# A two-layer trunk on one core: layer 0 gets four seven-product pairs and modulation vectors 2 to 5 as VectorE dot products

## The chip, the cores and the metric

The kernel runs on one core of one Trainium2 chip. The time is device microseconds of one execution. TensorE (PE) multiplies; VectorE (DVE) and ScalarE (ACT) work on the results, GpSimd (POOL) and SyncE (SP) mostly issue transfers.

## What is computed

Two layers over T = 640 tokens, 128 of context and 512 of latent, D = 1024, feed-forward width 4096. Each layer takes six modulation vectors from two conditioning vectors, `c` for latent tokens and `c_ctx` for context tokens:

```python
mod = silu(c)[None] @ w_mod[l] + b_mod[l]           # the same with c_ctx
sh1, sc1, g1, sh2, sc2, g2 = split(mod, 6)          # vectors 0 to 5
h = rmsnorm(x, norm1_g) * (1 + sc1) + sh1
branches = attention, convolution, pooling, gated unit   # all from h @ w_in
merged = sum(sigmoid(h @ w_gate[i] + b_gate[i]) * (branches[i] @ w_branch[i]))
x = x + g1 * (merged @ w_out)
h = rmsnorm(x, norm2_g) * (1 + sc2) + sh2
x = x + g2 * (square(relu(h @ w_mlp_in)) @ w_mlp_out)
```

So vector 2 is first needed at the end of the mixers, vectors 4 and 3 at the second norm, vector 5 by the MLP's output.

## The kernel before

Activations lie with channels on the partitions and tokens along the columns, in tiles of 128 x 640; TensorE takes them in two halves of 320 columns (`HALVES`). Every operand is split into a high and a low part: ScalarE copies to the high part (L240), VectorE subtracts (L241). One k-step of a product is three matmuls per half: high by high, high by low, low by high (`step`, L362). An output tile (`mtile`) is eight k-steps, 48 matmuls, or four, 24, for a half slab.

Weights come in slabs of 128 x 1024 in the order of `ORDER`, by SyncE's queue into a ring of four `raw` tiles; `use` takes the next slab, and keeps the splits of three ahead. TensorE and SyncE run in the order in which the code is written (`manual_schedule`). VectorE does too from the convolution's taps to the second gate tile of gate(1) (`byhand`); elsewhere a scheduler orders VectorE and ScalarE by priorities, which `later` shifts.

A layer runs: input projections; attention, woven on TensorE with two convolution inputs and gate(0) as filling (`fill`, `_weave`); the gated unit's projection `sgu_v` and branch(0); gate(3), branch(3), gate(2), branch(2), gate(1), branch(1); the output projection; the MLP. The convolution's 31 taps (L973) are spread over the gates as VectorE work, and its norm (`conv_out`, with sums over channels on TensorE, L414) falls into gate(1). The gate activation is line 1132 (ScalarE), the gate product line 1144 (VectorE). In attention the score maximum is line 848, the exponent 849, the normalising 850 and 851; the transposed probabilities arrive in `pt` (L857), which in attention is one bank, and are split by L240 and L241.

Modulation vectors 0 and 1 of layer 0 are made at the start. Its vectors 2 to 5 are made by `mod_steps`, on TensorE: 128 matmuls (L447) and 16 transposes (L454), handed out by `tick` in the gates and branches between gate(3) and branch(1). The vectors of layer 1 are made by `mod_dots` on VectorE during layer 0's MLP: 48 blocks, each with two dots of 1024 elements (L490) against a transposed slab of `w_mod`; `side` holds such a generator, `tick` moves it one block and `flush` runs it out.

The MLP of layer 1 (`fast_mlp`) computes 13 pairs of input tiles by a seven-product scheme (L653): eight block products become seven, at the price of sums and differences. The weights' sums are made by `Feed`, the activations' differences of quarters `ta` and `tb` by VectorE at L627 to L638, early, while TensorE has plain tiles. The MLP of layer 0 is plain, in four blocks of eight input tiles.

## Time and profile before

| | us |
|---|---|
| median of three runs | 2318.97 (2317.82 to 2321.76) |
| the profiled execution | 2326.15 |
| its span | 2324.4 |
| TensorE busy | 2254.2 (97%) |
| VectorE busy | 1655.0 (71%) |
| ScalarE busy | 856.4 (37%) |

Every stretch and duration below is of the profiled execution, which took 7.2 us more than the median. A row that is busy for 50 of 50 us shows an engine without a gap; since matmuls overlap, the distance from start to start tells what one costs. The same holds for VectorE, whose rows without dependence overlap somewhat. In a row's end, "[0.82 <-ACT h L240]" is the idle time before it and what ended it.

### The profile page before, as it was taken

To read this page: it belongs to the slowest core of one execution; us is meant where nothing else is said; L and a number is where in the kernel's file an instruction comes from. 1 tells how busy PE (TensorE), PEld (TensorE's weight loads), DVE (VectorE), ACT (ScalarE), POOL (GpSimd) and SP (SyncE) were. 2 spreads that over 40 slices of the span, in tenths; PEclk is the share of its full clock that TensorE was granted. 3 is DMA by queue.
4 is the path that set the end of the run, shared out by engine and by line. 5 is a ranking of instruction groups with operands and counts; after the bars stand their busy time and mean duration, and the time that the engine had idled before them with its cause. 6 is when DMAs were issued, how large, how long until landed. Compare 5 with 4: busy or idle time off the path is not lost.

```text
span 2324.4 us, 36290 instructions
## 1 busy us (share of the span) xinstructions
PE 2254.2 (97%) x15050; PEld 2182.7 (94%) x15050; DVE 1655.0 (71%) x2557; ACT 856.4 (37%) x1296; POOL 70.4 (3%) x188
## 2 busy tenths in 40 slices
PE   6999999999999999999999999999999999999997
PEld 5989899989999999999998898999999999999987
DVE  6676457678777776766477773687897788777776
ACT  5455342222335332222254553422224453232233
POOL 1100000000000000000011000000000000000001
PEclk9999999999999999999999999999999999999999
DMA  7421122333343444444354212222222432222223
GB/s 285 113 84 60 63 70 99 133 136 136 126 138 127 154 154 146 151 148 146 108 175 107 78 46 69 73 78 64 65 76 92 150 109 65 73 85 89 73 91 110
DMA packets 77253, 252.43 MB, mean 109 GB/s; under 512 B 11808, under 2 KB 12832, under 8 KB 76960
## 3 DMA queue, kind: packets, MB, share of 16 engines
q1 hardware_dynamic: 66592, 224.56, 29.9%
q0 software_dynamic: 9920, 24.89, 3.8%
q8 instruction: 118, 1.93, 0.3%
q10 hardware_dynamic: 576, 0.66, 0.1%
q14 instruction: 47, 0.39, 0.1%
HBM read 238.65 MB, written 10.75 MB: 107 GB/s over the span
## 4 chain that ended last, share of the span: by engine, by line
PE 66%; issue 24%; DVE 6%; ACT 2%; DMA 1%; POOL 0%; SPq 0%; DVEq 0%; ACTq 0%; POOLq 0%
PE ps L362 44%; PE ph L362 5%; PE pt L653 4%; DVE l L241 2%; PE sc L653 2%; PE pt L857 1%; PE sc L846 1%; PE po L865 1%; PE sc L362 1%; ACT h L240 1%; PE po L653 1%; PE sc L1031 1%; DMA st<-in_w_mod 1%; PE pt L447 1%; PE sc L414 1%
## 5 line engine op out<-in xcount | busy, mean ns | idle before, releaser
L362 PE MATMUL ps<-h,h 128*128 128x320 f32 x5296 | 1119.3, 310 | 12.8 <-ACT gx L1132 4.7
L362 PEld LDWEIGHTS ps<-h,h 128*128 128x128 f32 x5296 | 862.7, 188 | 31.9 <-ACT h L240 12.5
L362 PE MATMUL ps<-h,l 128*128 128x320 f32 x3408 | 835.7, 309 | 0.0
L240 ACT ACTIVATE h<-raw 128x1024 fp32r<-128x1024 f32 x337 | 357.2, 1060 | 976.7 <-PE ps L362 658.8
L362 PEld LDWEIGHTS ps<-h,l 128*128 128x128 f32 x3408 | 585.6, 188 | 0.0
L241 DVE TENSOR_TENSOR l<-raw,h 128x1024 fp32r<-128x1024 f32 x337 | 411.6, 1222 | 217.5 <-ACT h L240 217.1
L362 PE MATMUL ps<-l,h 128*128 128x320 f32 x1520 | 384.6, 308 | 0.0
L362 PEld LDWEIGHTS ps<-l,h 128*128 128x128 f32 x1520 | 263.9, 188 | 0.3
L973 DVE SCALAR_TENSOR_TENSOR cv<-cv,cw,cv 128x655 f32<-128x655 f32 x240 | 215.9, 899 | 6.1
L554 DVE SCALAR_TENSOR_TENSOR x<-ps,mod,x 128x128 f32<-128x128 f32 (+2 forms) x260 | 99.8, 434 | 117.9 <-PE ps L362 117.8
L362 PE MATMUL ph<-h,h 128*128 128x320 f32 x768 | 179.6, 318 | 0.0
L362 PEld LDWEIGHTS ph<-h,h 128*128 128x128 f32 x768 | 129.1, 188 | 7.2
L240 ACT ACTIVATE h<-tmp 128x640 fp32r<-128x640 f32 (+1 forms) x92 | 67.5, 737 | 138.7 <-DVE tmp L1311 79.9
L362 PE MATMUL ph<-h,l 128*128 128x320 f32 x384 | 118.5, 309 | 0.0
L362 PE MATMUL ps<-bo,h 128*128 128x320 f32 x512 | 96.5, 309 | 1.8 <-DVE mg L1144 1.8
L241 DVE TENSOR_TENSOR l<-pt,h 128x512 fp32r<-128x512 f32 x84 | 57.9, 689 | 41.5 <-ACT h L240 41.3
L362 PEld LDWEIGHTS ps<-bo,h 128*128 128x128 f32 x512 | 80.2, 188 | 5.1 <-DVE mg L1144 2.4
L241 DVE TENSOR_TENSOR l<-tmp,h 128x640 fp32r<-128x640 f32 x92 | 74.9, 816 | 8.3 <-ACT h L240 8.3
L240 ACT ACTIVATE h<-pt 128x512 fp32r<-128x512 f32 x84 | 50.3, 599 | 77.1 <-PE pt L857 70.8
L490 DVE SCALAR_TENSOR_TENSOR junk<-raw,sw 128x1024 f32<-128x1024 f32 x48 | 58.8, 1224 | 25.4 <-DMA raw<-in_w_modt 25.2
L653 PE MATMUL pt<-h,h 128*128 128x320 f32 x260 | 71.4, 309 | 2.6 <-DVE tmp L659 2.6
L362 PEld LDWEIGHTS ph<-h,l 128*128 128x128 f32 x384 | 72.1, 188 | 0.0
(300 smaller groups left out, 2573.9 us busy)
## 6 DMA issues: line engine op xcount, KB each, us to landing
raw<-in_slabs SPq DMA_DIRECT2D x324, 512.0 KB, 3.6
raw<-in_w_modt SPq DMA_DIRECT2D x48, 512.0 KB, 3.7
md<-in_w_mod SPq DMA_DIRECT2D x32, 512.0 KB, 4.4
q<-qd POOLq DMA_DIRECT2D x18, 256.0 KB, 3.1
st<-in_w_mod SPq DMA_DIRECT2D x8, 512.0 KB, 9.7
raw<-in_w_mod SPq DMA_DIRECT2D x8, 512.0 KB, 7.1
x<-in_x SPq DMA_DIRECT2D x8, 320.0 KB, 6.0
qd<-h POOLq DMA_DIRECT2D x8, 320.0 KB, 9.1
```

The source lines that it names most:

```text
L240: act.activation(h, src, AF.Copy)
L241: (eng or vec).tensor_tensor(lo, src, _f(h), ALU.subtract)
L362: pe.matmul(v[:, c0:c1] if half is None else v, w_[:, kk, :], x_[:, c0:c1], start=first and pi == 0, stop=last and pi == 2)
L414: pe.matmul(v[:, c0:c1], ones, src[:, c0:c1], start=True, stop=True)
L447: pe.matmul(t[32 * q:32 * q + 32], sv3[:, 2 * kp + i, :], rr[i][j], start=kp == 0, stop=kp == 3)
L490: vec.scalar_tensor_tensor(out, w, 0.5, s3[s], ALU.mult, ALU.mult, accum_out=dst[:, c, s:s + 1])
L554: vec.scalar_tensor_tensor(xc[:, c0:c1], v[:, c0 - b0:c1 - b0], gv[:, c, s:s + 1], xc[:, c0:c1], ALU.mult, ALU.add)
L653: pe.matmul(v, w_[:, k0 + k, :], x_, start=k == 0 and pi == 0, stop=k == 3 and pi == 2)
L846: pe.matmul(v[:, c0:c1], lq, kk[:, SEQ + c0:SEQ + c1], start=pi == 0, stop=pi == 1)
L857: pe.transpose(pt[:, qt * P:(qt + 1) * P], parts[hd, qt][:, j * P:(j + 1) * P], ident)
L865: pe.matmul(po, vt[:, 1 + j, hd // 4, :], halves[hd, j][pi], start=j == 0 and pi == 0, stop=j == 4 and pi == 1)
L973: vec.scalar_tensor_tensor(y, b[:, j:j + CO], cw[:, c * CONV_K + j:c * CONV_K + j + 1], y, ALU.mult, ALU.add)
```

## The change

Four things are changed.

1. `mod_steps` is removed. Layer 0's vectors 2, 4, 3, 5 are made by `mod_dots`, in 32 blocks. For layer 0 a block is two dots of 512 into a small pair, an addition of the pair, and one dot of 1024 (there is no `junk` tile for a second one). Two ticks stand behind each of two convolution inputs and eight gate tiles in `fill`, so in attention; one in each product of branch(0) and, as before, in the later gates. While VectorE is ordered by hand (`hold`), ticks do nothing; the rest follows in gate(1).
2. Layer 0's MLP is `paired_mlp`: 24 input tiles plain, each with half a slab of output products behind it, then four seven-product pairs (`PLAIN = (24, 6)`). Layer 1 keeps its 13 pairs and its early differences; layer 0 makes them (`sums`) behind the plain part, after the dots of layer 1 are flushed and their room is closed.
3. In layer 0 the square of the relu moves from VectorE to ScalarE, and the residual of the MLP's output is added in two pieces (128 and 512 columns) instead of three.
4. The scratch for dynamic transfers is halved.

```diff
-FAST = (1,)
+PLAIN = (24, 6)
...
+    for j in range(4, PLAIN[l]):
+        r += [("i", j), ("h", j // 4 - 1, j % 4)]
+    for b, p, fs in PAIRS[l]:
+        r += [("i", 4 * b + 2 * p + i) for i in range(2)] + [("h", *f) for f in fs]
+    return r + 2 * [("f", 3, m) for m in range(8)]
...
-    def mod_steps(l, g, mk):
...
+    def mod_dots(l, mp, vs, src, junk=None):
...
         for i, (n, c) in enumerate(blocks):
             wn = fetch(*blocks[i + 1]) if i + 1 < len(blocks) else None
+            dst = mod3(l, vs[n])
+            if junk:
+                dot(junk(), w, s3[0], dst[:, c, 0:1])
+            else:
+                acc = small(2)
+                for hf in range(2):
+                    cs = slice(512 * hf, 512 * hf + 512)
+                    dot(tmp(512), w[:, cs], s3[0][:, cs], acc[:, hf:hf + 1])
+                vec.tensor_tensor(dst[:, c, 0:1], acc[:, 0:1], acc[:, 1:2], ALU.add)
+            dot(w, w, s3[1], dst[:, c, 1:2])
...
-        while side:
+        while side and not hold[0]:
...
+    def paired_mlp(l, h, ss1, ab, fslot, relu2, es):
...
+        for j in range(4, PLAIN[l]):
+            b, i = divmod(j, 4)
+            v = relu2(_run(mtile(use("i", j), h)))
+            fs_.setdefault(b, []).append(v)
+            tick()
+            if keep and j == 4:
+                quarters = sums()
+            w = use("h", b - 1, i)
+            for m in (2 * i, 2 * i + 1):
+                out_plain(w, m, fs_[b - 1])
+                if m % 2 or j % 2:
+                    tick()
+        if not keep:
+            flush()
+            dots.close()
+            open_room()
...
+        ta, tb = quarters or sums()
...
+                if l == 0:
+                    side.append(mod_dots(0, mx, (2, 4, 3, 5), "w_modt0"))
                 def fill():
                     for c in range(2, 4):
                         ys.append((yield from conv_in(l, c, h, cv)))
+                        for _ in range(2):
+                            tick()
                     for m in range(KC):
                         yield from gate(0, m, h, gs, True)
+                        for _ in range(2):
+                            tick()
...
+                hold[0] = True
...
                         _run(gate(1, m, h, gs))
+                        hold[0] = m < 2
...
+                if l + 1 < DEPTH:
+                    act.activation(r, r, AF.Square)
+                else:
+                    vec.tensor_tensor(r, r, r, ALU.mult)
...
-    nc = _bacc.Bacc("TRN2", target_bir_lowering=False, num_devices=1, dynamic_dma_scratch_size=4096)
+    nc = _bacc.Bacc("TRN2", target_bir_lowering=False, num_devices=1, dynamic_dma_scratch_size=2048)
```

Three places show how the order of the instructions moves. A row is the line, the operation, what it writes and reads, and its shape; numbers behind names tell tiles apart. The lines of the changed file differ from those of before: L238 is the split, L446 a dot, L460 the addition of a pair, L861 the score maximum, L863 and L864 the normalising.

VectorE in attention of layer 0, from the 21st score maximum (`sm` from `sc`) to the next, before:

```order
L848 TENSOR_REDUCE sm427_2123<-sc426_2118 128x1
L881 TENSOR_TENSOR bo217_1218<-tmp383_1924,bo216_1217 128x512
L241 TENSOR_TENSOR l432_2139<-pt430_2133,h431_2138 128x512
L848 TENSOR_REDUCE sm439_2162<-sc438_2157 128x1
L241 TENSOR_TENSOR l435_2149<-raw401_2000,h434_2148 128x1024
L850 RECIPROCAL sm428_2124<-sm428_2124 128x1
L241 TENSOR_TENSOR l444_2178<-pt442_2172,h443_2177 128x512
```

Nothing but attention's own steps and one weight split stands between the maxima.

The same place after the change:

```order
L861 TENSOR_REDUCE sm449_2175<-sc448_2170 128x1
L460 TENSOR_TENSOR mod0_78<-sm456_2200 128x1
L446 SCALAR_TENSOR_TENSOR raw419_2043,mod0_78<-raw419_2043,sw298_1551 128x1024
L446 SCALAR_TENSOR_TENSOR tmp497_2361,sm495_2358<-raw459_2207,sw298_1551 128x512
L238 TENSOR_TENSOR l454_2191<-pt452_2185,h453_2190 128x512
L460 TENSOR_TENSOR mod0_78<-sm460_2209 128x1
L446 SCALAR_TENSOR_TENSOR raw455_2198,mod0_78<-raw455_2198,sw298_1551 128x1024
L238 TENSOR_TENSOR l465_2219<-raw423_2052,h464_2218 128x1024
L894 TENSOR_TENSOR bo217_1218<-tmp397_1958,bo216_1217 128x512
L861 TENSOR_REDUCE sm469_2232<-sc468_2227 128x1
```

Two dots of 1024, one of 512 and two additions of pairs have moved between the maxima; the split of `pt` (`l454`) comes behind the first two dots.

VectorE at the end of the convolution in layer 0, from the last sum of the taps (`c`, needed by TensorE's sum over channels) to the squares, before:

```order
L983 TENSOR_TENSOR c944_5898<-c944_5898,cv900_5459 128x655
L1212 TENSOR_SCALAR cw_83<-cols1_81 128x124
L241 TENSOR_TENSOR l965_6054<-raw952_5966,h964_6053 128x1024
L988 TENSOR_TENSOR cv716_3795<-cv716_3795,sc958_6033 128x655
L988 TENSOR_TENSOR cv754_4190<-cv754_4190,sc958_6033 128x655
L988 TENSOR_TENSOR cv856_5038<-cv856_5038,sc958_6033 128x655
L988 TENSOR_TENSOR cv900_5459<-cv900_5459,sc958_6033 128x655
L460 TENSOR_TENSOR mod0_78<-tmp951_5964 128x8 x2
L422 TENSOR_TENSOR sq959_6037<-sq959_6037,sq960_6040 128x655
```

Here the only foreign rows are the two small additions (L460) of `mod_steps`.

The same place after the change:

```order
L996 TENSOR_TENSOR c993_5944<-c993_5944,cv962_5553 128x655
L1226 TENSOR_SCALAR cw_83<-cols1_81 128x124
L460 TENSOR_TENSOR mod0_78<-sm1061_6345 128x1
L446 SCALAR_TENSOR_TENSOR raw1051_6277,mod0_78<-raw1051_6277,sw298_1551 128x1024
L1001 TENSOR_TENSOR cv810_4008<-cv810_4008,sc1012_6081 128x655
L1001 TENSOR_TENSOR cv841_4382<-cv841_4382,sc1012_6081 128x655
L1001 TENSOR_TENSOR cv925_5157<-cv925_5157,sc1012_6081 128x655
L1001 TENSOR_TENSOR cv962_5553<-cv962_5553,sc1012_6081 128x655
L446 SCALAR_TENSOR_TENSOR tmp1071_6412,sm1070_6411<-raw1060_6343,sw298_1551 128x512
L446 SCALAR_TENSOR_TENSOR tmp1072_6414,sm1070_6411<-raw1060_6343,sw298_1551 128x512
L419 TENSOR_TENSOR sq1013_6085<-sq1013_6085,sq1014_6088 128x655
```

Those additions have gone; a dot of 1024 has moved ahead of the subtraction of the mean (L1001) and two of 512 ahead of the squares (L419).

VectorE in layer 0's MLP at the evictions of two output tiles of a block (`x` from `ps`), before:

```order
L554 SCALAR_TENSOR_TENSOR x1024_6581<-ps1427_9428,mod0_78,x1024_6581 128x128
L554 SCALAR_TENSOR_TENSOR x1024_6581<-ps1427_9428,mod0_78,x1024_6581 128x192
L554 SCALAR_TENSOR_TENSOR x1024_6581<-ps1427_9428,mod0_78,x1024_6581 128x320
L241 TENSOR_TENSOR l1432_9488<-raw1424_9422,h1431_9487 128x1024
L490 SCALAR_TENSOR_TENSOR junk1447_9671,mod1_79<-raw1440_9606,sw1195_7571 128x1024
L490 SCALAR_TENSOR_TENSOR raw1440_9606,mod1_79<-raw1440_9606,sw1195_7571 128x1024
L554 SCALAR_TENSOR_TENSOR x1025_6582<-ps1433_9491,mod0_78,x1025_6582 128x128
L554 SCALAR_TENSOR_TENSOR x1025_6582<-ps1433_9491,mod0_78,x1025_6582 128x192
L554 SCALAR_TENSOR_TENSOR x1025_6582<-ps1433_9491,mod0_78,x1025_6582 128x320
```

The evictions have splits and dots between them, and no other work.

After the change, VectorE at the end of the plain part, up to the last split of `ta`:

```order
L630 TENSOR_TENSOR tmp1658_10491<-h1147_6761,h1148_6762 128x320
L607 TENSOR_TENSOR tmp1655_10482<-tmp1655_10482,h1140_6754 128x320
L238 TENSOR_TENSOR l1652_10475<-tmp1650_10470,h1651_10474 128x640
L608 TENSOR_TENSOR tmp1655_10482<-tmp1657_10484,tmp1655_10482 128x320
L238 TENSOR_TENSOR l1654_10479<-tmp1647_10461,h1653_10478 128x640
L610 TENSOR_TENSOR tmp1657_10484<-tmp1657_10484,tmp1656_10483 128x320
L631 TENSOR_TENSOR tmp1658_10491<-tmp1658_10491,tmp1655_10482 128x320
L632 COPY tmp1658_10491<-tmp1657_10484 128x320
L238 TENSOR_TENSOR l1660_10496<-tmp1658_10491,h1659_10495 128x640
L238 TENSOR_TENSOR l1662_10500<-tmp1655_10482,h1661_10499 128x640
```

The differences (L605 to L632) and their splits now run up to `l1662`.

TensorE there after the change: the end of the first product of the first pair (`pt`), and the start of the second (`po`), which reads the splits `h1637` to `l1662`.

```order
L677 MATMUL pt1663_10503<-h1139_6753,h1620_10394 128x320
L677 MATMUL pt1663_10503<-h1140_6754,h1620_10394 128x320
L677 MATMUL pt1663_10503<-h1139_6753,l1621_10395 128x320
L677 MATMUL po1665_10518<-h1637_10436,h1622_10398 128x320
L677 MATMUL po1665_10518<-l1638_10437,h1622_10398 128x320
L677 MATMUL po1665_10518<-h1637_10436,l1623_10399 128x320
L677 MATMUL po1665_10518<-h1645_10457,h1622_10398 128x320
```

Between the end of `pt` and the rows of `po` no other product stands in TensorE's order.

## Rows read from the trace of the kernel before

**Rows 1.** The page, part 1: busy time, share of the span, and instructions of each engine.

```profile
PE 2254.2 (97%) x15050; PEld 2182.7 (94%) x15050; DVE 1655.0 (71%) x2557; ACT 856.4 (37%) x1296; POOL 70.4 (3%) x188
```

**Rows 2.** Busy by stretch: both layers' MLP; PE, PEld, DVE, ACT, POOL, clock, DMA, GB/s.

```profile
800.00:850.00 50.00, 50.00 (x343) 50.00 (x342) 35.50 (x53) 17.47 (x22) 0.00 (x0) 1.00 0.49 151
1900.00:1950.00 50.00, 50.00 (x343) 50.00 (x343) 46.67 (x86) 20.18 (x26) 0.00 (x0) 1.00 0.25 78
```

**Rows 3.** Line 447, the modulation matmuls: nanoseconds (least, median, most), first and last start.

```profile
L447 PE MATMUL pt<-md,silu x128: 592/605/617, 385.5 to 608.7; 128*32 128x512 f32 x128
```

**Rows 4.** Lines 1132 and 1144 in layer 0 and layer 1: first and last start.

```profile
L1132 ACT ACTIVATE gx<-ps,bgh x24: 774/778/782, 372.2 to 648.1; 128x640 f32<-128x640 f32 x24
L1144 DVE SCALAR_TENSOR_TENSOR gx<-gx,ps x24: 812/816/822, 459.4 to 675.9; 128x640 f32<-128x640 f32 x24
...
L1132 ACT ACTIVATE gx<-ps,bgh x24: 774/777/782, 1528.9 to 1787.2; 128x640 f32<-128x640 f32 x24
L1144 DVE SCALAR_TENSOR_TENSOR gx<-gx,ps x24: 814/817/822, 1610.9 to 1815.0; 128x640 f32<-128x640 f32 x24
```

**Rows 5.** Timeline of VectorE (start, length): dot of 1024, split of 640, next dot.

```profile
823.91 1.22 DVE L490 SCALAR_TENSOR_TENSOR junk<-raw,sw 128x1024 f32<-128x1024 f32 x1
...
825.05 0.82 DVE L241 TENSOR_TENSOR l<-tmp,h 128x640 fp32r<-128x640 f32 x1
825.79 1.22 DVE L490 SCALAR_TENSOR_TENSOR raw<-raw,sw 128x1024 f32<-128x1024 f32 x1
```

**Rows 6.** Timeline of VectorE in attention: a row of 512 and the next.

```profile
126.26 0.69 DVE L899 TENSOR_TENSOR tmp<-tmp,sm 128x512 f32<-128x512 f32 x1
126.86 0.16 DVE L850 RECIPROCAL sm<-sm 128x1 f32<-128x1 f32 x1
```

**Rows 7.** Busy by stretch: attention of layer 0.

```profile
119.20:272.00 152.80, 145.93 (x972) 138.41 (x973) 103.87 (x183) 81.95 (x172) 5.69 (x10) 1.00 0.21 66
```

**Rows 8.** Timeline of VectorE: score maxima 9 and 29 of layer 0.

```profile
148.19 0.82 DVE L848 TENSOR_REDUCE sm<-sc 128x1 f32<-128x640 f32 x1
...
230.72 0.82 DVE L848 TENSOR_REDUCE sm<-sc 128x1 f32<-128x640 f32 x1
```

**Rows 9.** Waits from 119 to 272: us in total, times, longest.

```profile
ACT h L240 <- PE pt L857: 35.4, 25, 2.6
```

**Rows 10.** Busy by stretch: before and into the first branch product.

```profile
302.50:332.00 29.50, 28.59 (x195) 28.32 (x194) 24.12 (x37) 16.15 (x29) 0.00 (x0) 1.00 0.21 72
```

**Rows 11.** Busy by stretch: layer 1, end of the convolution up to branch 1.

```profile
1752.80:1792.53 39.73, 39.73 (x266) 39.05 (x265) 28.05 (x40) 21.75 (x26) 0.56 (x1) 1.00 0.22 75
```

**Rows 12.** Timeline of layer 1: sums over channels on TensorE and what precedes them on VectorE.

```profile
1752.84 0.84 DVE L983 TENSOR_TENSOR c<-c,cv 128x655 f32<-128x655 f32 x1
1755.88 1.26 PE L414 MATMUL sc<-c,ones_c 128*128 128x328 f32 x4
1761.00 2.72 DVE L422 TENSOR_TENSOR sq<-sq,sq 128x655 f32<-128x655 f32 x3
1764.03 1.26 PE L414 MATMUL sc<-sq,ones_c 128*128 128x328 f32 x4
```

**Rows 13.** Timeline of VectorE: differences of quarters in layer 1, four and the next.

```profile
1909.94 1.69 DVE L627 TENSOR_TENSOR tmp<-f,h 128x320 f32<-128x320 f32 x4
1911.55 0.48 DVE L635 TENSOR_TENSOR tmp<-f 128x320 f32<-128x320 f32 x1
```

**Rows 14.** Busy by stretch around idle TensorE; the granted clock is third from the end.

```profile
1256.00:1258.00 2.00, 1.31 (x4) 0.55 (x3) 0.00 (x0) 1.37 (x2) 0.00 (x0) 0.50 0.70 105
1258.00:1260.00 2.00, 2.00 (x7) 1.30 (x6) 0.00 (x0) 0.71 (x2) 0.00 (x0) 0.50 0.83 120
1260.00:1262.00 2.00, 2.00 (x11) 2.00 (x10) 1.38 (x3) 1.14 (x3) 0.00 (x0) 0.60 0.61 187
1262.00:1264.00 2.00, 2.00 (x16) 2.00 (x14) 1.97 (x4) 1.61 (x2) 0.00 (x0) 1.00 0.54 181
```

**Rows 15.** The page, part 5: dots of layer 1's vectors; busy, mean ns | idle before.

```profile
L490 DVE SCALAR_TENSOR_TENSOR junk<-raw,sw 128x1024 f32<-128x1024 f32 x48 | 58.8, 1224 | 25.4 <-DMA raw<-in_w_modt 25.2
```

More of the change, by code (lines that the diff above doesn't have):

```diff
@@ L55, with _pairs @@
 BR_ORDER = (0, 3, 2, 1)
-FAST = (1,)
-def _pairs():
-    due = [(b, mp) for b in range(6) for mp in range(4)]
+PLAIN = (24, 6)
+def _pairs(plain):
+    due = [(b, mp) for b in range(6) for mp in range(4)][plain - 4:]
     take = {(6, 1): 1, (7, 0): 1, (7, 1): 0}
     r = []
-    del due[:2]
-    for b in range(1, 8):
-        for p in range(1 if b == 1 else 0, 2):
-            n = take.get((b, p), 2)
-            r.append((b, p, due[:n]))
-            del due[:n]
+    for i in range(plain // 2, 16):
+        b, p = divmod(i, 2)
+        n = take.get((b, p), 2)
+        r.append((b, p, due[:n]))
+        del due[:n]
     assert not due
     return r
-PAIRS = _pairs()
+PAIRS = [_pairs(n) for n in PLAIN]
 def _order(l):
@@ L102 @@
 assert all(len(r) == NS for r in ORDER)
+ENDS = [l * NS + ORDER[l].index(("h", (PLAIN[l] - 1) // 4 - 1, (PLAIN[l] - 1) % 4)) for l in range(DEPTH)]
 C_BMOD, C_N1, C_N2, C_BG = 0, 48, 56, 64
@@ L273, in trunk, with __init__ @@
     class Feed:
-        def __init__(self, mp):
+        def __init__(self, mp, end):
+            self.end = end
             self.w2 = maker(mp, "wh2", 1, 1024), maker(mp, "wl2", 1, 1024)
@@ L280, in __init__ @@
             self.todo, self.n, self.done = [], 0, set()
-            self.base = nxt["use"]
-            self.slab = self.base
+            self.slab = nxt["cap"] + 1
             self.got = {}
         def load(self, upto):
-            while self.slab < min(upto, len(order)):
+            while self.slab < min(upto, self.end):
                 l, s = order[self.slab]
@@ L496, in trunk @@
     side = []
-    taps = [iter(())]
+    taps, hold = [iter(())], [False]
     def tick(n=0):
@@ L608, in fast_mlp @@
             todo.append(fd.pair(i, [i + 2 + n for n in range(len(fs))]))
             i += 2 + len(fs)
-        fd.tail = {n: fd.plain(n) for n in range(i, len(order))}
-        f = [relu2(v) for v in vs]
-        f.append(relu2(_run(mtile(use("i", 3), h))))
-        f1 = [relu2(_run(mtile(use("i", 4), h)))]
-        def plain_tile(w, m, fb):
-            v = _run(mtile(w, fb, k0=4 * (m % 2)))
-            for half in range(2):
-                residual(x[m], v[:, HALVES[half][0]:], mod3(l, 5), m, half)
@@ L621, in fast_mlp @@
[L621 to L639 removed]
+        fd.tail = {n: fd.plain(n) for n in range(i, fd.end)}
@@ L684, in out_tile @@
                 fb, m, n, k = due.pop(0)
-                plain_tile(tuple(z.rearrange("p (k c) -> p k c", c=P) for z in ready[n]), m, fs_[fb])
+                out_plain(tuple(z.rearrange("p (k c) -> p k c", c=P) for z in ready[n]), m, fs_[fb])
                 if m % 2:
@@ L1303, in trunk @@
         with opened(f"ml{l}") as mp:
-            fast = l in FAST
-            fslot = maker(mp, "f", 16 if fast else 32, T)
+            fslot = maker(mp, "f", 16, T)
+            es = ExitStack()
             def relu2(v):
@@ L1310, in relu2 @@
                     act.activation(r, v, AF.Relu)
-                vec.tensor_tensor(r, r, r, ALU.mult)
+                if l + 1 < DEPTH:
+                    act.activation(r, r, AF.Square)
+                else:
+                    vec.tensor_tensor(r, r, r, ALU.mult)
                 return split(r, fslot, T)
-            def mlp_in(b):
-                out = []
-                if b == 0:
-                    out += [relu2(v) for v in first([("i", j) for j in range(3)], h, ss1, ab)]
-                for j in range(len(out), 8):
-                    out.append(relu2(_run(mtile(use("i", 8 * b + j), h))))
-                    tick()
-                return out
-            if l + 1 < DEPTH:
-                side.append(mod_dots(l + 1, mp))
-            f = fast_mlp(l, mp, h, ss1, ab, fslot, relu2) if fast else mlp_in(0)
-            for b in range(0 if fast else 3):
-                fn = mlp_in(b + 1)
-                for m in range(KC):
-                    v = _run(mtile(use("f", b, m), f))
-                    for half in range(2):
-                        residual(x[m], v[:, HALVES[half][0]:], mod3(l, 5), m, half)
-                    tick()
-                f = fn
-            flush()
+            f = paired_mlp(l, h, ss1, ab, fslot, relu2, es)
             if l + 1 < DEPTH:
@@ L1344, in trunk @@
             feed.clear()
+            es.close()
+            if l + 1 < DEPTH:
+                nxt["dma"] = nxt["split"] = (l + 1) * NS
+                nxt["cap"] = ENDS[l + 1]
     main.close()
```

183 lines of the change are left out of this document (80 added, 103 removed).

## The prediction

> **What bounds the kernel now.** The page's busy shares come first: TensorE is busy for 97% of the span and VectorE for 71% [rows 1]. A share over the whole span hides stages, so the next view is the table by stretch. In layer 0's MLP TensorE is busy for 50.00 of 50 us and VectorE for 35.50; in layer 1's MLP, which already has seven-product pairs, VectorE stands at 46.67 of 50, with TensorE still full [rows 2]. So VectorE can be filled to about 93% without a wait of TensorE where its work comes in small, independent pieces. Attention is different: from 119.2 to 272 TensorE is busy for 145.93 of 152.80 us, VectorE for 103.87 [rows 7], and the waits there are short steps from engine to engine: ScalarE waits 35.4 us in 25 pieces for a transposed tile `pt` [rows 9]. The span is set by TensorE nearly everywhere, by such handovers in attention. A step off TensorE is therefore gain at its full length, if nothing that replaces it makes TensorE wait.
>
> **The sum starts from the profiled execution**, 2326.15 us; the median of the three runs, 2318.97, is 7.2 us lower, and the forecast is the median plus the sum.
>
> **Removed: the modulation matmuls.** Line 447 issues 128 matmuls of 605 ns between 385 and 609 us [rows 3], in row-tiled groups of four side by side. What they cost is read best by comparing the layers, since layer 1 runs the same gates and branches without them. From the first gate activation (line 1132) to the last gate product (line 1144) layer 0 takes 675.9 - 372.2 = 303.7 us, layer 1 takes 1815.0 - 1528.9 = 286.1 [rows 4]. The difference, **17.6 us**, is what leaves TensorE's path, if VectorE keeps up as it does in layer 1.
>
> **Removed: 48 matmuls.** Where TensorE is full it runs 343 matmuls of 320 columns in 50 us [rows 2], 145.8 ns each. A pair of input tiles is 96 products of this size plain and 84 with seven products. Four pairs save 48 x 0.1458 = **7.0 us**. Together the gain is 24.6 us.
>
> **Added: 32 dot blocks on VectorE.** One block is two dots of 512, one of 1024 and a small addition. A dot of 1024 has the next row start 825.05 - 823.91 = 1.14 us later [rows 5]; a row of 512 has its successor 126.86 - 126.26 = 0.60 us later [rows 6]. A block takes 2 x 0.60 + 1.14 + 0.17 (estimate for the small addition from the 0.16 us of the reciprocal in rows 6) = 2.5 us, all 32 take 80 us. The rows show durations longer than these distances, 1.22 and 0.69 us; the distances count, since rows without a dependence overlap. (The Trainium skill, VectorE: DVE Perf Modes, section "The TRN2 errata", says that a VectorE instruction that reads SBUF pays a fixed extra latency between instructions, so that fewer, larger tiles are better: a rule against splitting one dot of 1024 in two. Taken with the durations, a block would be 2 x 0.69 + 1.22 + 0.17 = 2.8 us and the dots 8 us longer. By rows 5 and 6 the split costs 0.06 us a block.)
>
> Where these 80 us go is told by the changed order of VectorE.
>
> *Attention, 14 blocks.* A head takes four score maxima (line 848). The 9th starts at 148.19 and the 29th at 230.72 [rows 8]: five heads in 82.5 us, 16.5 each. Adding the distances of all rows of VectorE between these two maxima in the order gives 57 us before and 88 us after, of which 30 are dots; the heads hold 16.2, 17.2, 16.4, 19.2 and 18.7 us. The work no longer fits: at full occupancy the five heads need 88 - 82.5 = 5 us more, and that is the least. Here VectorE is a link of a chain (score maximum, exponent on ScalarE, normalising, transpose, split), a dot in front of a link holds the transposed tile, and `pt` is one bank whose next turn waits for the split. So full occupancy isn't reached. At 93%, the value of layer 1's MLP [rows 2], 88 us of work take 94.6, +12; at 85% they take 103, +21. I take **+13**, near the row, and keep 5 to 25. Before the change the same stretch ran at 69%.
>
> *Behind attention, 8 blocks.* Four fall beside the gated unit's projections, where VectorE has little to do; four (10 us) beside the first branch product. From 302.5 to 332 VectorE is busy for 24.12 of 29.5 us [rows 10], so 5.4 us are free and 4.9 are too many. I take **+4**, bounds 0 and 8: the values that the next products wait for are queued behind the dots on VectorE.
>
> *End of the convolution, 9 blocks* (one more lies in the taps). They take 22.5 us between the last taps and branch 1. The same stretch of layer 1, 1752.80 to 1792.53, has VectorE busy for 28.05 of 39.73 us [rows 11], so 11.7 us are free and 10.8 too many. How much reaches TensorE depends on its fixed order. The sum of squares over channels stands at 1755.88, 2.2 us after the sum that it needs (L983 ends at 1753.7), and again at 1764.03, 0.3 us after its squares (1761.00 + 2.72) [rows 12]. TensorE thus has hardly any slack at the second place, and dots queue ahead of both. I take **+9**, bounds 4 and 16.
>
> *MLP of layer 0, plain part.* The dots of layer 1's vectors wait for their weights as before (25.2 us in all) [rows 15] and must now end after 24 input tiles, not 32. Per input and output slab (96 matmuls, 14.0 us) the order holds 9.7 to 13.7 us of VectorE work; ScalarE takes over the squaring. That is at most 97%: **+2**, bounds 0 and 10.
>
> **Added: a stop before the pairs.** The seven products need eight tiles of differences of quarters. In layer 1 they are made early, while TensorE has plain tiles to run. In layer 0 they are emitted after the last plain tile, and the order of VectorE shows the consequence: behind the eviction of the last plain output tile (`x1116`) there are 35 further rows up to the split `l1662`, 17.4 us by distances (rows of 320 are (1911.55 - 1909.94) / 4 = 0.40 us apart [rows 13], splits of 640 0.74 [rows 5]). TensorE has one product of 12 matmuls, 1.75 us, that needs none of it; its next, `po1665`, needs the differences from `h1637` to `l1662`. Nothing else is in TensorE's order to cover the stop. It comes to 17.4 - 1.8 + 1 to 2 us for the eviction and the handovers with ScalarE, some 17 us. Around 1256 TensorE idles for a third of the time, its granted clock stands at 0.50, the lower of its two levels (1.2 and 2.4 GHz), and stays there for two us of full work and at 0.60 in the mean of the next two, before it is full again [rows 14]; that costs 2 x 0.50 + 2 x 0.40 = 1.8 us. **+19**, bounds 16 and 22.
>
> **The sum:** -24.6 + 13 + 4 + 9 + 2 + 19 = **+22.4**, so 2341 us, 1.0% slower. All low bounds give -24.6 + 25 = 0.4 (2319), all high ones -24.6 + 81 = 56 (2375); neither is likely whole. The forecast's own range is 2326 to 2353.
>
> **The rivals.**
>
> *1. TensorE's work decides (faster).* VectorE's 29% of idle time takes up all dots, and the differences are ready in time. Then the time falls by the work that leaves TensorE, 24.6 us: 2294. For it speaks that TensorE is busy for 97%, and that layer 1's MLP hides VectorE at 93%. Against it, the order puts the differences behind the last plain tile. Chance 0.04. (The Trainium skill, Perfetto Trace Analysis, section "Identifying the Most-Contended Engine", says to judge TensorE by the busy share of its weight loads and to improve the engine with the highest share first. That share is 94% here [rows 1], and by the rule the work taken from TensorE is the gain.)
>
> *2. The dots fit, only the stop costs.* Waits between dots and chain overlap so well that attention loses its least, 5, the end of the convolution 4 and the rest nothing, with a stop of 16 to 19: 25 to 28 against 24.6, so 2319 to 2322. If the five heads also smooth out over the two at each end, attention loses nothing and it is 2314 or a little under. For it: 82.5 us of head time before hold 25 us of idle VectorE. Against it: a chain of handovers without slack. Chance 0.20.
>
> *3. Dots starve the slabs (slower still).* Dots read from the same ring of four `raw` tiles as the weight slabs, through SyncE's queue in program order. A dot that VectorE runs late holds its tile, the next slab's load waits behind it, and TensorE, which wants a slab every 7 us, waits for its split. This decides from the point where VectorE is behind by more than two tiles, about 5 us, which attention reaches. Then attention runs at 85% (+21), and the other terms are near their upper ends (7 + 14 + 6 + 21): 2319 - 24.6 + 69 = 2363. Chance 0.15.
>
> *4. The change doesn't do what it says there:* the stop is covered, because TensorE still has queued tiles when VectorE reaches the differences. Then 19 us fall away: 2322. The order of TensorE, in which only 12 matmuls lie between, speaks against it. Chance 0.05.
>
> **How the numbers follow.** The forecast has the remaining 0.56. A measurement of this kernel tells about 0.2%, 4.6 us, from no change: 2314.3 to 2323.6. Faster: rival 1 and a quarter of rival 2, 0.09. Same: the rest of rival 2 without its upper edge and rival 4, about 0.16. Slower: 0.75. The range reaches from rival 2, 2317, to rival 3, 2363, which leaves out rival 1, the low edge of 2 and half of 3.
>
> **What would show it.** Attention: the distance of the 9th from the 29th score maximum, 82.5 us before, should be 93 to 97. The stop: TensorE idle for 15 to 20 us before the first `po` product of layer 0, with VectorE in the lines of the quarter differences, and a clock of 0.5 behind it. Convolution: the span from the first gate activation to the last gate product in layer 0 near 286 + 13. Layer 1 should be unchanged. The forecast is wrong in its largest term if TensorE is busy before the pairs, and in its least certain one if attention keeps 82.5 us.

## The result, and the profile after

The changed kernel takes 2374.94 us (median of four runs, 2371.82 to 2380.19) against 2318.85 before (now of four runs, too): 1.0242 times as long, 95% interval 1.0220 to 1.0264. It is 2.4% slower, 56 us, where 22 were forecast.

The page of the changed kernel, part 1, answers to [rows 1]:

```profile
PE 2241.4 (95%) x14858; PEld 2177.6 (92%) x14858; DVE 1773.5 (75%) x2823; ACT 881.4 (37%) x1330; POOL 70.5 (3%) x188
```

192 matmuls are gone: 128 modulation matmuls, 16 transposes and 48 of the MLP. The work did leave, but TensorE is busy for only 12.8 us less and the span is 45.5 us longer, so that TensorE idles for 58 us more. Where, is read by landmarks that both traces have: the first score maximum, the first gate product of branch 0, the first mixing product of the gated unit, the first gate activation, the last gate product, the first query projection of layer 1, the end.

| stretch | before | after | difference | forecast |
|---|---|---|---|---|
| up to the first score maximum | 120.8 | 116.8 | -4.0 | 0 |
| attention, gated unit's projection | 183.0 | 206.1 | +23.1 | +13 |
| branch 0 | 32.5 | 32.6 | +0.1 | +4, with the next |
| gated unit's output | 35.9 | 41.1 | +5.2 | |
| gates, convolution, branches 3 to 1 | 303.7 | 306.6 | +2.9 | -8.6 |
| output projection and MLP | 578.7 | 602.4 | +23.7 | +14 |
| layer 1 | 1069.8 | 1064.3 | -5.5 | 0 |

The first and last rows are mostly a difference of the two profiled executions: that of before was 7.2 us over its median, that of the changed kernel 3.1 under. In all ten kernels below layer 1 takes 1064.2 to 1066.9 whatever they change, and the start varies between 116.4 and 120.8. The middle rows add up to 55.0, against 56.1 between the medians.

**Attention.** The table by stretch, from the 9th to the 29th score maximum [rows 8], first of the kernel before, then of the changed one (TensorE, weight loads, VectorE, ScalarE, GpSimd; the granted clock is third from the end):

```profile
148.19:230.72 82.53, 79.81 (x534) 75.89 (x533) 58.44 (x104) 44.67 (x89) 2.39 (x4) 1.00 0.19 58
```

```profile
144.21:244.39 100.18, 86.83 (x543) 81.11 (x542) 85.37 (x188) 47.68 (x93) 2.38 (x4) 0.95 0.33 101
```

The five heads take 17.65 us more. TensorE idles 100.18 - 86.83 = 13.35 us instead of 2.72, that is 10.6 more; and it is busy 7.0 us longer, 1.3 of it for nine more matmuls that fall into the stretch, 5.7 for the same work at a granted clock of 0.95 instead of 1.00. TensorE's waits for the split of `pt`, over all of layer 0's attention (us in total, times, longest; before, then changed), grow from 0.9 to 15.9 us:

```profile
PE pt L857 <- DVE l L241: 0.9, 2, 0.7
```

```profile
PE pt L870 <- DVE l L238: 15.9, 10, 2.5
```

One such place of the changed kernel, VectorE, then TensorE, then the table in steps of 2 us:

```profile
224.23 0.67 DVE L446 SCALAR_TENSOR_TENSOR tmp<-raw,sw 128x512 f32<-128x512 f32 x1
...
226.06 0.68 DVE L446 SCALAR_TENSOR_TENSOR tmp<-raw,sw 128x512 f32<-128x512 f32 x1
...
226.75 0.80 DVE L861 TENSOR_REDUCE sm<-sc 128x1 f32<-128x640 f32 x1
227.47 0.68 DVE L238 TENSOR_TENSOR l<-pt,h 128x512 fp32r<-128x512 f32 x1
```

```profile
228.29 1.09 PE L870 MATMUL pt<-ident,p 128*128 128x128 f32 x4 [2.38 <-DVE l L238]
```

```profile
226.00:228.00 2.00, 0.00 (x0) 0.00 (x0) 2.00 (x7) 0.42 (x1) 0.00 (x0) 1.00 0.03 12
228.00:230.00 2.00, 1.71 (x8) 1.74 (x9) 2.00 (x6) 0.99 (x3) 0.00 (x0) 0.55 0.00 0
230.00:232.00 2.00, 2.00 (x9) 1.81 (x9) 2.00 (x6) 0.60 (x2) 0.00 (x0) 0.60 0.61 213
232.00:234.00 2.00, 2.00 (x17) 2.00 (x16) 0.98 (x2) 0.28 (x1) 0.00 (x0) 1.00 0.81 307
```

Four dots of 512 stand ahead of a score maximum and of the split of `pt`. The next transpose into the one `pt` bank waits 2.38 us for that split, and behind the wait TensorE does 17 matmuls in 4 us where it does 17 in 2 us afterwards. The wait costs its length and then 1.7 us again (0.45 x 2 + 0.40 x 2).

**The gates.** The rows that answer to [rows 4], layer 0 of the changed kernel:

```profile
L1145 ACT ACTIVATE gx<-ps,bgh x24: 774/777/796, 396.6 to 668.4; 128x640 f32<-128x640 f32 x24
...
L1157 DVE SCALAR_TENSOR_TENSOR gx<-gx,ps x24: 808/816/823, 478.6 to 703.2; 128x640 f32<-128x640 f32 x24
```

703.2 - 396.6 = 306.6 us: without one modulation matmul the stretch is longer than with them, 20.5 over the 286.1 of a layer without them. Two stops hold most of it. VectorE, TensorE, and the table around both:

```profile
631.68 0.69 DVE L446 SCALAR_TENSOR_TENSOR tmp<-raw,sw 128x512 f32<-128x512 f32 x1 [1.00 <-DMA raw<-in_w_modt]
...
632.91 0.83 DVE L996 TENSOR_TENSOR c<-c,cv 128x655 f32<-128x655 f32 x1
```

```profile
633.80 2.55 PE L411 MATMUL sc<-c,ones_c 128*128 128x328 f32 x4 [7.93 <-DVE c L996]
```

```profile
626.00:634.00 8.00, 0.20 (x1) 0.20 (x2) 7.00 (x15) 1.35 (x2) 0.00 (x0) 0.81 0.41 134
634.00:638.00 4.00, 4.00 (x12) 3.17 (x13) 2.70 (x5) 0.74 (x1) 0.00 (x0) 0.53 0.33 119
668.00:672.00 4.00, 1.01 (x5) 0.75 (x6) 4.00 (x8) 1.97 (x3) 0.00 (x0) 0.99 0.40 128
672.00:680.00 8.00, 6.97 (x29) 6.17 (x29) 5.05 (x10) 1.99 (x3) 0.10 (x1) 0.58 0.24 83
```

The sum over channels waits 7.93 us for the last sum of the taps, ahead of which dots stand (VectorE waits 3.4 us for their weights besides). In the 12 us of the first two rows TensorE does 13 matmuls, 1.9 us of work at 0.146: 10.1 lost. Around 670, at the start of branch 1's product, three more blocks (657 to 671) stand among the rows that make its input, and TensorE waits for a split:

```profile
671.55 0.62 PE L359 MATMUL ps<-l,h 128*128 128x320 f32 x2 [2.48 <-DVE l L238]
```

It does 34 matmuls in the 12 us of the last two rows: 7.0 lost. Together 17.1 of 20.5.

**The MLP.** The stop before the pairs, the table and TensorE's `po` product:

```profile
1084.00:1104.00 20.00, 7.38 (x22) 4.64 (x22) 17.81 (x38) 6.58 (x11) 0.00 (x0) 0.61 0.09 26
1104.00:1108.00 4.00, 4.00 (x25) 4.00 (x24) 0.68 (x2) 0.00 (x0) 0.00 (x0) 0.82 0.00 0
```

```profile
1085.98 0.41 PE L677 MATMUL po<-h,h 128*128 128x320 f32 x1 [0.97 <-ACT h L237]
1089.00 0.63 PE L677 MATMUL po<-l,h 128*128 128x320 f32 x1 [2.60 <-DVE l L238]
...
1102.65 0.64 PE L677 MATMUL po<-l,h 128*128 128x320 f32 x1 [0.33 <-DVE l L238]
```

24 us with 47 matmuls, 6.9 us of work: 17.1 us lost, each pair of splits waited for in turn. But 23.7 + 7.0 (the matmuls saved) - 17.1 leaves 13.6 us elsewhere. VectorE and TensorE in the plain part, then VectorE's waits for the dots' weights, which answer to [rows 15], and TensorE's for evictions:

```profile
892.57 1.23 DVE L446 SCALAR_TENSOR_TENSOR junk<-raw,sw 128x1024 f32<-128x1024 f32 x1 [2.80 <-DMA raw<-in_w_modt]
...
894.46 1.00 DVE L590 SCALAR_TENSOR_TENSOR x<-ps,mod,x 128x128 f32<-128x128 f32 x2
```

```profile
895.61 0.82 PE L359 MATMUL ps<-h,h 128*128 128x320 f32 x4 [1.90 <-DVE x L590]
```

```profile
DVE junk L446 <- DMA raw<-in_w_modt: 53.9, 38, 2.9
...
PE ps L359 <- DVE x L590: 7.4, 8, 1.9
```

VectorE stands for 2.80 us in front of a dot whose weights have not landed; the eviction behind it is late, and TensorE waits for the bank, 7.4 us in eight places. Output tiles of four k-steps come every 3.5 us now, those of before, of eight, every 7, and the wait for dots' weights is 53.9 us instead of 25.2.

### The profile page after: what moved, and what is told of

The parts are those of the page before. It is cut to its first block, busy times and chain, and to the rows that moved or that the text cites. A ratio compares the mean times of both kernels' runs of the same rounds, so it can differ in the third digit from the quotient of the medians.

```text
span 2369.9 us, 36208 instructions
## 1 busy us (share of the span) xinstructions
PE 2241.4 (95%) x14858; PEld 2177.6 (92%) x14858; DVE 1773.5 (75%) x2823; ACT 881.4 (37%) x1330; POOL 70.5 (3%) x188
## 5 line engine op out<-in xcount | busy, mean ns | idle before, releaser
L359 PE MATMUL ps<-h,h 128*128 128x320 f32 x5040 | 1073.1, 311 | 23.6 <-DVE x L590 7.4
L359 PEld LDWEIGHTS ps<-h,h 128*128 128x128 f32 x5040 | 824.3, 189 | 35.7 <-issue 11.3
L359 PE MATMUL ps<-h,l 128*128 128x320 f32 x3280 | 808.5, 309 | 0.0
L359 PEld LDWEIGHTS ps<-h,l 128*128 128x128 f32 x3280 | 566.0, 188 | 0.0
L238 DVE TENSOR_TENSOR l<-raw,h 128x1024 fp32r<-128x1024 f32 x341 | 416.4, 1221 | 162.2 <-ACT h L237 162.1
L590 DVE SCALAR_TENSOR_TENSOR x<-ps,mod,x 128x128 f32<-128x128 f32 x192 | 96.6, 546 | 39.9 <-PE ps L359 39.9
L237 ACT ACTIVATE h<-tmp 128x640 fp32r<-128x640 f32 (+1 forms) x100 | 72.7, 735 | 87.5 <-DVE tmp L726 27.3
L446 DVE SCALAR_TENSOR_TENSOR junk<-raw,sw 128x1024 f32<-128x1024 f32 x48 | 58.8, 1225 | 54.2 <-DMA raw<-in_w_modt 53.9
L677 PE MATMUL pt<-h,h 128*128 128x320 f32 x340 | 93.8, 310 | 5.0 <-DVE tmp L683 5.0
L446 DVE SCALAR_TENSOR_TENSOR raw<-raw,sw 128x1024 f32<-128x1024 f32 x80 | 97.6, 1220 | 1.1
L238 DVE TENSOR_TENSOR l<-tmp,h 128x640 fp32r<-128x640 f32 x100 | 81.3, 818 | 11.8 <-ACT h L237 11.8
L238 DVE TENSOR_TENSOR l<-pt,h 128x512 fp32r<-128x512 f32 x84 | 57.7, 687 | 36.6 <-ACT h L237 36.5
L677 PE MATMUL pt<-h,l 128*128 128x320 f32 x272 | 84.0, 309 | 0.0
```

The lines of the kernel that those rows point to most:

```text
L237: act.activation(h, src, AF.Copy)
L238: (eng or vec).tensor_tensor(lo, src, _f(h), ALU.subtract)
L359: pe.matmul(v[:, c0:c1] if half is None else v, w_[:, kk, :], x_[:, c0:c1], start=first and pi == 0, stop=last and pi == 2)
L446: vec.scalar_tensor_tensor(out, w, 0.5, z, ALU.mult, ALU.mult, accum_out=acc)
L590: vec.scalar_tensor_tensor(x[m][:, c0:c1], v[:, c0:c1], mod3(l, 5)[:, m, s:s + 1], x[m][:, c0:c1], ALU.mult, ALU.add)
L677: pe.matmul(v, w_[:, k0 + k, :], x_, start=k == 0 and pi == 0, stop=k == 3 and pi == 2)
```

## The experiments

**The two parts apart.** In `pairs_only` layer 0's vectors are made by `mod_steps` as before, the MLP is the changed one; `dots_only` is the kernel before with the 32 dot blocks and their ticks. Their core, the first against the changed kernel, the second against the kernel before:

```diff
-                    side.append(mod_dots(0, mx, (2, 4, 3, 5), "w_modt0"))
...
+                    side.extend([mod_steps(l, 1, md), mod_steps(l, 2, md)])
```

```diff
+                    side.append(mod_dots0(0, mx, (2, 4, 3, 5), "w_modt0"))
...
-                    side.extend([mod_steps(l, 1, md), mod_steps(l, 2, md)])
```

> Layer 0's vectors 2 to 5 on TensorE as before, the MLP with four pairs as after the change. If the MLP's loss is its own (the stop before the pairs, and evictions held up behind dots that wait for their weights), the stretch from the last gate product to layer 1 stays 24 us longer than before, the attention and the gates are as before, and the time is 2319 + 24 - 3 to 6 (layer 1 was that much shorter) = 2337 to 2343. If much of it is carried over from the mixers, the time is 2319 - 7 + 17 (the stop alone) = 2329 or less.

> The kernel before with layer 0's vectors 2 to 5 as 32 dot blocks on VectorE, the plain MLP kept. If the losses of the two parts add up, attention is 23 us longer, the gated unit 5, the gates 3 in spite of the matmuls taken out, the start up to 4 shorter: 2319 + 27 to 31 = 2346 to 2350. If the start's 4 us have another cause than the dots, the upper end. If the two parts of the change make each other worse, under 2342.

2344.05 us (1.0103, 1.0076 to 1.0130) and 2350.57 (1.0119, 1.0093 to 1.0145), each about 1 us over its range. Against the median of 2318.99 they are 25.1 and 31.6 us longer, 56.6 together (by the ratios 24 and 28): the parts add up, and each is slower alone. By stretch, `pairs_only` has 183.0, 303.7 and 606.4 in attention, gates and MLP; `dots_only` has 206.4, 306.7 and 578.2. So the MLP's loss is its own (it is 4.0 us larger here than in the changed kernel, 2.3 of them in the stop and behind it), and the dots lose 31.6 us over the 17.6 that they save.

**Do the dots' loads hold things up?**

```diff
         def fetch(n, c):
-            t = raw_tile()
-            sp.dma_start(out=t, in_=a[src][n, c])
-            return t
+            return s3[1]
```

> The changed kernel with all dots reading a tile that is already there in place of a weight slab (the modulation vectors are wrong by that, the work on VectorE is the same but for layer 0's 1024-wide dot, now two of 512 and an addition, 2.7 us a block for 2.5). Theory 1, VectorE is too full in attention and every stop also lowers the clock: attention stays 20 us or more over before. Theory 2, the dots' loads hold ring tiles and their waits block VectorE: attention falls to within 10 us of before. In layer 0's plain MLP part the waits of dots for their weights go, so if these hold up the evictions, the 9 us that TensorE loses there fall to 3 or less.

2375.73 us in one run. Attention takes 213.7, not less than 206.1 but 7.6 more: the dots' loads are not its cause, and a tenth more work in the dots is paid in full and more. The trace of the changed kernel says the same of the slabs. In all of attention ScalarE, which splits them first, waits for a slab once:

```profile
ACT h L237 <- DMA raw<-in_slabs: 1.1, 1, 1.1
```

This settles the third rival's place: no starved slabs in attention. In the MLP's plain part it is the other way. The table for the same 20 us, first the changed kernel, then this one:

```profile
880.00:900.00 20.00, 18.10 (x124) 17.87 (x123) 14.17 (x23) 4.63 (x6) 0.00 (x0) 1.00 0.48 148
```

```profile
880.00:900.00 20.00, 20.00 (x139) 20.00 (x138) 18.48 (x30) 7.31 (x9) 0.00 (x0) 1.00 0.28 79
```

VectorE is busier, 18.48 of 20, and TensorE has no gap. The MLP's stretch falls from 602.4 to 592.9, by 9.5, and TensorE's waits for these evictions are all but gone. There most of the loss was not a lack of VectorE's time, but its standing in front of a load, with evictions behind.

**The stop moved.**

```diff
-            if keep and j == 4:
+            if j == (4 if keep else 16):
                 quarters = sums()
```

> The changed kernel with layer 0's differences of quarters made in the plain part (at input tile 16), as in layer 1. If the stop before the pairs is what the trace shows, 16.6 us with its stretch at the lower clock, it goes and the time falls from 2375 to 2358 to 2362; the differences' 20 us of VectorE work then delay evictions by 0 to 4 us. If VectorE is too full there, it only moves the loss: a fall of under 8.

2369.17 us (1.0206, 1.0185 to 1.0226): 5.8 less, the second case. The stop is gone, but the differences stand together behind tile 16, and the table there, of `early_sums`, shows what they push aside:

```profile
980.00:1000.00 20.00, 15.14 (x102) 14.67 (x101) 19.87 (x38) 3.49 (x4) 0.00 (x0) 1.00 0.48 140
1000.00:1020.00 20.00, 15.36 (x83) 14.87 (x82) 18.91 (x37) 7.57 (x11) 0.00 (x0) 0.83 0.42 127
```

VectorE is full for 40 us, evictions come late, and TensorE idles for 9.5 us and loses some of its clock. The MLP takes 598.8.

**What the clock takes of a stop.** TensorE repeats the first product of the pair, so that it is busy while it waits. `fill_once` is shown; `fill_stop` has `10 if not keep and not fs_.get(b)`.

```diff
+            for _ in range(9 if not keep and (b, p) == (6, 0) else 0):
+                prod("pt", q["w1"], 0, b11)
             p1, r1 = prod("pt", q["w1"], 0, b11), tmp(TH)
```

> The changed kernel with the first product of layer 0's first pair issued eleven times instead of once (the last result counts), 120 more matmuls, 17.5 us, all inside the stop in which TensorE waits for the differences. If the stop is set by VectorE alone, these cost nothing, TensorE's clock stays at its upper level, and the stretch of the MLP falls by the clock's share, 1.5 to 3 us, from 602.4 to about 600. If the stop is shorter than read, or the clock makes nothing, it stays or grows.

> As fill_stop, whose repeats stood before two of the four pairs, not one: here nine repeats, 108 matmuls, before the first pair of layer 0 alone. In fill_stop such a matmul took 0.16 us, so these take 17.5 us, within the 19.6 us from the last plain matmul to full speed in the changed kernel. If the clock's fall is part of the stop's price, the MLP's stretch falls from 602.4 by 1.5 to 3 us although TensorE does 17.5 us more work. If not, it stays within 1 us, or grows where the repeats outlast the stop.

`fill_stop` took 2398.53 us, the MLP 629.3: its repeats stood before two pairs, the second without a stop to hide in, so it says little. `fill_once` took 2379.85, the MLP 608.0, 5.6 longer: by the number the second case, but not for the reason given there; its parts are clearer. From the pair's first product to its next `pt` product it takes 26.9 us (1084.51 to 1111.38), the changed kernel 24.7 (1083.09 to 1107.80), with 16 us more work on TensorE. ScalarE's timeline in `fill_once` shows why it isn't less:

```profile
1101.69 0.74 ACT L237 ACTIVATE h<-tmp 128x640 fp32r<-128x640 f32 x1 [2.75 <-DVE tmp L632]
1105.49 0.44 ACT L707 ACTIVATE tmp<-pt 128x320 f32<-128x320 f32 x1 [3.06 <-PE pt L677]
1105.82 0.73 ACT L237 ACTIVATE h<-tmp 128x640 fp32r<-128x640 f32 x1
```

The copy of `pt`, now ready only after all repeats, stands ahead of the last copy for the differences: the chain itself got 3.3 us longer. From the last wait of the `po` product to the next `pt` product the changed kernel needs 1107.80 - 1102.65 = 5.15 us, this one 1111.38 - 1107.46 = 3.92, its clock at 1.00 throughout: 1.2 us is the clock's price here. Of the other 3.4 us of the 5.6, 3.2 lie behind the stop, and the two traces show where. One product waits for a split for 1.86 us in both (up to 1185.41 in the changed kernel, up to 1188.99 in `fill_once`). Behind it the clock stays up in the first and falls in the second:

```profile
1184.40:1192.40 8.00, 6.99 (x47) 6.99 (x48) 2.37 (x4) 1.56 (x3) 0.00 (x0) 1.00 0.34 107
```

```profile
1188.00:1196.00 8.00, 7.01 (x29) 7.01 (x30) 1.67 (x2) 0.57 (x1) 0.00 (x0) 0.57 0.31 109
```

29 matmuls instead of 47 are 2.6 us at 0.146 each. The same wait costs its length in one kernel and more than twice that in the other.

**Half as many dots in attention.**

```diff
-                        for _ in range(2):
-                            tick()
+                        tick()
```

> The changed kernel with one tick, not two, behind each filling of attention: about 7 blocks in attention instead of 14; the others fall to the end of the convolution. By occupancy, five heads then hold some 72 us of VectorE work for 82.5: attention, 183.0 before and 206.1 changed, comes to 186 to 191. If it is the place of a dot in front of a link that counts, and not the load, half the loss stays: 193 to 196. The gates get 7 to 8 more blocks, 18 to 20 us, and grow from 306.6 to 322 to 328.

2378.60 us in one run. Attention takes 191.3, just over the first case; the gates 321.8, the lower edge of what was expected, with ten more blocks and not 7 to 8. The MLP, which this edit leaves alone, takes 607.1. The five heads in the table of `one_tick`:

```profile
145.95:235.03 89.08, 81.97 (x534) 77.14 (x533) 70.91 (x139) 46.73 (x92) 2.38 (x4) 0.98 0.26 76
```

Five blocks of dots begin in these heads instead of 12 (the traces have 10 and 24 dots of 512 there), and they cost 6.5 us instead of 17.65. VectorE is busy for 71% of the time before, 80% here and 85% in the changed kernel: attention did not fill it further. TensorE's busy time is 2.2 us longer for as many matmuls, against 7.0. In the gates, where 2 blocks begin in `spread_dots` (below), 10 in the changed kernel and 20 here, the stretch is 288.8, 306.6 and 321.8: a block costs 2.2 us, then 1.5, of its own length of 2.5.

**The dots where VectorE has time.** `spread_dots` is `dots_only` with one tick in attention, one for every second step of the gated unit's projection, and two behind each of its outputs.

```diff
-                    vn, sw, sb = _run(sgu_v(l, h, mk))
+                    vn, sw, sb = ticked(sgu_v(l, h, mk), 2)
...
+                        sg.append(_run(sgu_out(g, vn, sw, sb, h)))
+                        tick()
+                        tick()
```

> The plain MLP, and the 32 blocks spread by where VectorE has time: one tick behind each filling of attention, one for every second step of the gated unit's projection, two behind each of its four outputs. If the loss is load over capacity stretch by stretch, attention is 186 to 191, the gated unit's parts 3 to 8 us longer together, the gates 290 to 296, and the time 2316 to 2324, where the dots as they were placed gave 2351. If every dot costs TensorE about its own share wherever it stands, it is still over 2340.

2325.24 us (1.0013, 1.0004 to 1.0023): 25 us better than `dots_only`, just over the range given. Attention with the projection takes 195.8, over the 186 to 191 expected (five heads 89.0, as in `one_tick`; ten blocks in the projection another 4.5), the unit's other parts 75.5 for 68.4, the gates 288.8 for 303.7. Fifteen us gained, twenty lost.

`half_dots` is the kernel before with 16 blocks, none in attention; `blocks` is the list in layer 1's `mod_dots`, which now begins with layer 0's vector 5.

```diff
+                    side.append(mod_dots0(0, mx, (4,), "w_modt0"))
...
-                    vn, sw, sb = _run(sgu_v(l, h, mk))
+                    vn, sw, sb = ticked(sgu_v(l, h, mk), 2)
+                    flush()
...
-                    side.extend([mod_steps(l, 1, md), mod_steps(l, 2, md)])
+                    side.append(mod_steps(l, 1, md))
...
+        blocks = [(l - 1, 5, c) for c in range(KC)] + [(l, v, c) for v in (1, 0, 2, 4, 3, 5) for c in range(KC)]
```

> The kernel before with only vectors 4 and 5 of layer 0 as dots, 16 blocks, none of them in attention or in the gates: vector 4 in the gated unit's projection, where VectorE is busy for a fifth of the time, vector 5 in front of layer 1's dots in the plain MLP; vectors 2 and 3 stay on TensorE. If a dot costs nothing where VectorE has time, half of the 17.6 us goes: gates 295, the unit's parts up to 3 longer, the MLP within 1 of 578.7, time 2310 to 2314. If the dots cost by themselves, it is 2317 or more.

2315.23 us (0.9986, 0.9974 to 0.9997), between the two cases. Its gates, by the rows of the lines that were 1132 and 1144:

```profile
L1173 ACT ACTIVATE gx<-ps,bgh x24: 771/777/782, 368.6 to 635.6; 128x640 f32<-128x640 f32 x24
L1185 DVE SCALAR_TENSOR_TENSOR gx<-gx,ps x24: 812/816/823, 455.9 to 663.4; 128x640 f32<-128x640 f32 x24
```

663.4 - 368.6 = 294.8, half of the 17.6 gone, and attention is 182.9: eight blocks in the projection, where VectorE was busy for 7.02 of 30 us (266 to 296 in the kernel before), cost nothing when attention leaves no backlog. The MLP, 581.8, is 3.1 longer than before. Most of that is one place, where dots again stand ahead of an eviction, with a lower clock behind it:

```profile
1122.23 0.38 PE L362 MATMUL ps<-h,h 128*128 128x320 f32 x1 [3.59 <-DVE x L595]
```

It is the one version that beats the kernel before, by 0.14%, near what can be told.

**Pairs without the stop and without the waits.** `better_pairs` is `pairs_only` with differences made one tile at a time within the plain part, and two tiles for the dots' weights beside the ring (for the room, layer 1's dots are split in two of 512 and one of 1024 as well).

```diff
+        ring = maker(mp, "dw", 2, D)
...
-            t = raw_tile()
+            t = ring()
...
+            elif not keep and j in (8, 11, 14, 17, 20):
+                next(made, None)
```

> Layer 0's vectors on TensorE as before, four pairs, with the differences of quarters made one tile at a time within the plain part (tiles 8 to 17), and the dots of layer 1 reading from two tiles of their own instead of the slabs' ring. If the MLP's loss is the stop and the dots' waits for their weights, the MLP's stretch, 578.7 before and 606.4 with the pairs alone, comes to 574 to 578 and the time to 2313 to 2317. If VectorE is too full for pairs in this layer, evictions stay late and it is 2322 or more.

2324.75 us (1.0017, 1.0005 to 1.0030): 19.3 better than `pairs_only`, but over the range given and in that of the second case; the MLP takes 582.7. Late evictions are not the main reason, though: in the plain part TensorE idles for 4.8 us, in the changed kernel for 9.7. The MLP is 4.0 us over before, 11.0 over what 48 matmuls less would give, and 4.9 of these are lost at one place at the start of the pairs (11.76 us for 47 matmuls), TensorE, then ScalarE, of `better_pairs`:

```profile
1049.94 0.64 PE L719 MATMUL pt<-h,l 128*128 128x320 f32 x1 [3.15 <-DVE l L238]
```

```profile
1042.43 1.06 ACT L237 ACTIVATE h<-raw 128x1024 fp32r<-128x1024 f32 x1 [0.69 <-DMA raw<-in_slabs]
1045.59 1.06 ACT L237 ACTIVATE h<-raw 128x1024 fp32r<-128x1024 f32 x1 [2.10 <-DMA raw<-in_slabs]
```

The pairs' first weight slabs are asked for only when the plain part is over; in the changed kernel the stop hid that. Without this place (3.15 us of wait and the clock behind it) the MLP would be near the 578.7 of before, still without the gain of 7.0; that was not run.

## Why the prediction was wrong

The direction was right and the places of the losses were named. The size was 56.1 us for 22.4, and the time lies outside both ranges, 2326 to 2353 and 2317 to 2363. The terms miss by 10.1 us in attention, 1.3 behind it, 11.5 at the end of the convolution, 11.6 in the plain MLP and -1.9 at the stop, together 32.6 of the 33.7. Three steps failed: a wait was priced at its length in attention, without the clock behind it; the free time at the convolution was read from the wrong stretch; and in the plain MLP the busy share was counted, and not the order. Step by step:

- *Gains.* 24.6 us less work on TensorE: not contradicted (`half_dots` shows half of the 17.6 as 303.7 - 294.8 = 8.9; the 7.0 rest on the 48 matmuls that are gone). Rival 1 failed: the gain of TensorE's work was not the kernel's gain.
- *Attention, +13 taken, +23.1 measured.* The 93% was not reached, nor the 93 to 97 us of the sign: the 88 us of VectorE's work by distances took 100.18, 88%. TensorE idles 10.6 us more in the five heads, near the 12 that 93% had given. The step that failed is that a wait was counted at its length. Behind three waits of 2.38 to 2.70 us TensorE's clock fell, and TensorE is busy for 5.7 us longer in the five heads; I had priced that once, at the stop, and not in attention. That the heads would be 5.7 us shorter without it is read from the trace; no run shows it. The other 5.4 us lie behind the 29th maximum, in the last heads and the projection, which the reading by five heads left out.
- *Behind attention, +4:* 5.3, right.
- *End of the convolution, +9 taken, bounds 4 to 16, measured 20.5.* The free time was read from the stretch behind the last tap [rows 11], 11.7 of 39.7 us. (The row at 1755.88 is the sum over `c`, not that of the squares.) But four of the nine blocks start among the last taps, where layer 1's VectorE is busy for 25.27 of 27.8 us (1725 to 1752.8), and three and a half of them stand ahead of the sum over channels: 7.93 us of wait, with the clock 10.1. The upper bound was too low because it was made from the wrong stretch.
- *Plain MLP, +2 taken, 10 the bound, measured about 13* (602.4 with the stop and the gain taken off). The sum asked how much of VectorE's time is used, up to 97%. What counted was order: an eviction behind a dot that waits for its load. `dots_no_load` gives back 9.5 of it with VectorE fuller than before. The other 4 are about as much as three waits of TensorE in and behind the pairs, 0.94, 0.96 and 1.86 us (up to 1144.08, 1177.81 and 1185.41), but no run took these away.
- *The stop, +19:* 17.1, right, and the only part where the order named each waiting row. The clock was low within the stop (0.61) more than behind it (0.82). Whether the loss goes away when the work moves was not claimed: moved in one piece it stays (`early_sums`), spread tile by tile most of it goes (`better_pairs`).
- *Rival 3* gave 2363, nearer to the measured time than the forecast, but by the wrong cause: the ring starved nobody in attention.
- *The sum of all high bounds, 2375,* equals the measured time by luck: two terms lie above their high bounds and three below.

## What to carry to other kernels

Work that is moved to an engine with idle time costs nothing only where no other engine waits for what stands behind it. Eight blocks in the gated unit's projection were free when attention left no backlog. In five heads of attention, where VectorE was busy for 71% before, the first five blocks cost 6.5 us for 12.5 of VectorE's time, and the next seven 11 for 14.5. A wait of the busiest engine should be priced at its length, and at its upper bound with what the clock may take behind it. And in an engine's fixed order every instruction that waits for a load holds all that stand behind it, so the place of such an instruction can matter more than the engine's busy share.
